# Turning the meta tokens' attention weights on the tensor engine instead of GpSimd and VectorE

## The chip, the cores and the metric

The kernel runs on one core of a Trainium2 chip, in one launch. The time is device microseconds; the figure given for a kernel is the median of its runs, and less is better. A core has a tensor engine (PE; its weight loads are listed apart as PEld), VectorE (DVE), ScalarE (ACT), GpSimd (POOL) and SyncE (SP), which issues the loads and stores. Each engine works through its own instructions in order, and waits for the others by semaphores. PE's results go to PSUM, a small memory of banks; the other engines copy them from there to SBUF.

## The reference, cut to what matters

One layer of a decoder over 512 tokens of width 1024, with 16 learned meta tokens put ahead of them (528 rows). A combined projection feeds a retention mixer, a stick-breaking attention mixer with 16 heads of width 64, and two gates; their merged output goes through an output projection and a gated FFN. The change touches the attention mixer alone:

```python
z = jnp.einsum('bhtd,bhsd->bhts', q_blk, k_pre) * scale
valid = (s_pos[None, :] < t_pos[:, None]) & (s_pos[None, :] >= PAD)
log_not = jnp.where(valid, jax.nn.log_sigmoid(-z), 0.0)
after = lax.cumsum(log_not, axis=3, reverse=True) - log_not
a = jnp.where(valid, jnp.exp(jax.nn.log_sigmoid(z) + after), 0.0)
outs.append(jnp.einsum('bhts,bhse->bhte', a, v_pre))
```

The sum over s runs over the 16 meta tokens and the 512 tokens. The meta tokens' part of it is what the change treats. All is float32.

## The kernel before

**Precision.** A float32 value is held as a pair of values, hi and lo, in the tensor engine's faster float32 type (F32R): `split` (L98) lets ACT copy the value into hi (L99) and DVE subtract hi from it for lo (`lo_of`, L96). A product then is three matmuls: hi by hi, hi by lo, lo by hi. All matmuls are recorded at L90 (`mm`), all transposes on PE at L93 (`turned`); these are matmuls whose stationary operand is the piece that is turned and whose moving operand is the identity.

**The attention stage** (s2, up to about 308 us of the span) walks over eight pairs of heads. For each head and each of four blocks of 128 queries, `score` makes z in a bank of PSUM (`bank_a`), two sigmoids on ACT (L641, L643, tiles sm and sp), a running product on DVE (the scan, L645) and a multiplication on DVE (L646). Its result, sp, holds the weights with queries down the 128 partitions and, along a row, first 16 meta tokens and then the block's tokens (144, 272, 400 or 528 columns).

The weights must be turned before they can be multiplied with the values. For the 512 tokens `turn` does it on PE in blocks of 128x128 into a bank of PSUM (`bank_b`, two banks, tile name pb) and splits the result into ah and al, of 128, 256, 384 or 512 columns. For the 16 meta tokens `turn_meta` does it in another way: GpSimd splits the 16 columns of each block into mg (L654, L655), one DVE instruction turns mg by blocks of 32x32 into x (L656), and GpSimd copies four pieces of x into am (L659). am holds, for both heads of a pair, 32 rows each: 16 of hi and 16 of lo. `values` starts with one matmul of am with vm, the meta tokens' values, and adds those of ah and al with vt; the result is in a `bank_b` too, and ACT (L680) and DVE (L681) move it to ysb.

**vm** is made by `Values.tail`, once for four heads: a projection of xmd, 64 columns that hold the meta tokens' hi, hi, lo, lo, so that the sum of two 32-row halves gives the values twice over; two splits then write 32 rows for each of the two heads of a pair. xmd is filled at the stage's start by four DVE copies. Another tile, xm, with 48 columns (hi, zeros, lo), is filled there as well, for other projections.

**What fills the gaps.** While a pair's attention is made, PE also does the projection for the next pair: q and k by `qk_work` (split on DVE as qa, qb, ka/kl, kb/kl), values (vt) in the pairs 2 to 5, and gates in some pairs. `merge` sets the order: a pair's 20 pieces (four scores z, four turns t, one tm for `turn_meta` and one pv for `values`, for each of the two heads, in the order of `seq`) are emitted one by one, and behind each a share of the projection's columns (`SHARES`). PE executes them in just this order, since `keep` pins it.

**GpSimd's other work.** In the pairs 1 to 5 it computes sums of the tokens' quarters, `token_sums` (tiles go, tl, at L170; six steps behind each tm; ACT makes th at L179), which the gates' products use. In the pairs 6 and 7 it combines the gates' weights in their buffer raw (`quarters_in_place`, L246 to L249). ACT and DVE then split these (wh, wl). The products of the gates are added on DVE into go (L592). All these stand in GpSimd's one queue in the order in which the program emits them, between the steps of `turn_meta`.

Of the kernel before, what the change touches and what calls it, by code (L numbers as in the profile page):

```python
# [10 lines left out]
F32 = mybir.dt.float32  # L11
F32R = mybir.dt.float32r
AF = mybir.ActivationFunctionType
ALU = mybir.AluOpType
PSUM = bass.MemoryType.PSUM

P = 128
NM = 16
T = 512
L = NM + T  # L20
NT = T // P
D = 1024
KD = D // P
RH, DK, DV = 4, 256, 512
SH, DH = 16, 64
# [9 lines left out]
def hybrid_block(  # L35
# [18 lines left out]
    nc = tc.nc  # L54
    x, out = x[0], out[0]
# [9 lines left out]
    def bank_p():  # L65
        return ps_p.tile([P, 512], F32, tag="p", name="pp")
# [4 lines left out]
    def bank_b():  # L71
        return ps_b.tile([P, 512], F32, tag="b", name="pb")
# [5 lines left out]
    ident = cst.tile([P, P], F32, name="ident")  # L78
# [6 lines left out]
    def keep(ins):  # L85

        return tc.keep_in_program_order(ins) if pinned[0] else ins

    def mm(*args, **kw):
        return keep(nc.tensor.matmul(*args, **kw))  # L90

    def turned(dst, src, idn):
        return keep(nc.tensor.transpose(dst, src, idn))  # L93

    def lo_of(lo, src, hi):
        nc.vector.tensor_tensor(lo, src, hi.bitcast(F32), op=ALU.subtract)  # L96

    def split(hi, lo, src):  # L98
        ins = nc.scalar.activation(hi, src, AF.Copy)  # L99
        if split_in_order[0]:  # L100
            tc.keep_in_program_order(ins)
        lo_of(lo, src, hi)
# [233 lines left out]
    hT = hn.tile([P, KD, L], F32R, name="hT")  # L336
    hL = hn.tile([P, KD, L], F32R, name="hL")
    xm = hn.tile([P, KD, 48], F32R, name="xm")
# [94 lines left out]
    with tc.tile_pool(name="s2", bufs=2, side=RS, reuse_waits="tile") as s2:  # L433
# [12 lines left out]
        vms = [s2.tile([P, 4, P], F32R, name=f"vm{i}", bufs=1) for i in range(2)]  # L446
        for vm in vms:
            nc.gpsimd.memset(vm.bitcast(F32), 0.0)
        xmd = s2.tile([P, KD, 64], F32R, name="xmd", bufs=1)
        NS = 3  # L450
        sms = []
        for i in range(NS):
            t = s2.tile([P, L + 2], F32, name=f"sm{i}", bufs=1)
            nc.gpsimd.memset(t[:, L : L + 2], 0.0)
            sms.append(t)
        both = s2.tile([P, T], F32R, tag="am", name="am", bufs=1)
        nc.gpsimd.memset(both.bitcast(F32), 0.0)
        ams = [both[32 * i : 32 * (i + 1)] for i in range(2)]

        vts = {}  # L460

        class Values:
# [18 lines left out]
                    split(vt[:, j, :, 0:DH], vt[:, j, :, DH:], pv)  # L481

            def tail(self, bank=bank_p):
                ps = bank()[:64, :256]
                k = 0
                for wh, wl in self.units:
                    for kk in range(4):
                        mm(ps, xmd[:, k, :], wh[:, kk, :], start=(k == 0), stop=False)
                        mm(ps, xmd[:, k, :], wl[:, kk, :], start=False, stop=(k == KD - 1))
                        k += 1  # L490
                        yield 2 * 256
                vs = s2.tile([32, 256], F32, tag="vs", name="vs", bufs=1)
                nc.scalar.activation(vs, ps[32:64], AF.Copy)
                nc.vector.tensor_tensor(vs, ps[0:32], vs, op=ALU.add)
                vv = vs.rearrange("p (h d) -> p h d", h=4)
                vm = vms[self.c % 2]
                for i in range(2):
                    v = vm[32 * i : 32 * (i + 1)]
                    split(v[:, i::2, 0:DH], v[:, i::2, DH:], vv[:, i::2, :])

            def first(self):
                return (self.load, lambda _: self.part((0, 1)))
# [144 lines left out]
            return sp  # L647

        def turn_meta(hd, att):

            g = s2.tile([P, NT, 32], F32R, tag="mg", name="mg", bufs=1)
            x = s2.tile([P, NT, 32], F32, tag="vs", name="x", bufs=1)
            for i in range(NT):
                nc.gpsimd.tensor_copy(g[:, i, 0:NM], att[i][:, 0:NM])  # L654
                nc.gpsimd.tensor_tensor(g[:, i, NM:], att[i][:, 0:NM], g[:, i, 0:NM].bitcast(F32), op=ALU.subtract)  # L655
            nc.vector.transpose(x.rearrange("p a b -> p (a b)"), g.rearrange("p a b -> p (a b)").bitcast(F32))  # L656
            am = ams[hd].rearrange("p (i b r) -> p i b r", i=NT, b=4)
            for b in range(4):
                nc.gpsimd.tensor_copy(am[:, :, b, :], x[32 * b : 32 * (b + 1)])  # L659

        def turn(j, att):
            w = T - j * P
# [26 lines left out]
        def pair(p):  # L689
# [9 lines left out]
            def tm(hd, j):  # L699
                turn_meta(hd, att[hd])  # L700

                if 1 <= p < 6:
                    for _ in range(6):
                        next(token_sums, None)
# [33 lines left out]
        def innorm(i):  # L738
            n = NM if i == NT else P
            c0 = 0 if i == NT else NM + i * P  # L740
            xt = xts[i]
            junk = bank_a().rearrange("p a b -> p (a b)")
            ss = cst.tile([P, 1], F32, name=f"ss{i}")
            nc.scalar.activation(junk[:n], xt[:n], AF.Square, accum_out=ss[:n])
            rstd_of(ss[:n], ss[:n], 1e-6, 1.0 / D, n)
            for j in range(2):
                hx = s2.tile([P, 512], F32, tag="qb", name="hx")
                cs = slice(512 * j, 512 * (j + 1))
                nc.vector.scalar_tensor_tensor(hx[:n], xt[:n, cs], ss[:n], gps[:n, j, :], op0=ALU.mult, op1=ALU.mult)
                pt = bank_b().rearrange("p (a b) -> p a b", a=4)  # L750
                for a in range(4):
                    turned(pt[:, a, :n], hx[:n, a * P : (a + 1) * P], ident[:n, :n])
                ks = slice(4 * j, 4 * j + 4)
                split(hT[:, ks, c0 : c0 + n], hL[:, ks, c0 : c0 + n], pt[:, :, :n])
# [19 lines left out]
        for j in range(NT):  # L774
# [2 lines left out]
                    pass  # L777
            if j + 2 <= NT:
                innorm(j + 2)
        for i, v in enumerate((hT, hT, hL, hL)):  # L780
            nc.vector.tensor_copy(xmd[:, :, 16 * i : 16 * (i + 1)], v[:, :, 0:NM].bitcast(F32))
        nc.vector.memset(xm[:, :, 16:32].bitcast(F32), 0.0)
        nc.vector.tensor_copy(xm[:, :, 0:16], hT[:, :, 0:NM].bitcast(F32))
        nc.vector.tensor_copy(xm[:, :, 32:48], hL[:, :, 0:NM].bitcast(F32))
# [36 lines left out]
    with tc.tile_pool(name="s3", bufs=1, side=RS, reuse_waits="tile") as s3:  # L821
# [10 lines left out]
        for f in range(0, KD, 2):  # L832
# [4 lines left out]
            for e in range(2):  # L837
                ps = bank_p()
# [95 lines left out]
    def ret_qk(h):  # L934
        uq = feat_units(w_in[:, O_RQ + DK * h : O_RQ + DK * (h + 1)])
        pq = bank_a()
        for e in range(2):
            feat_mm(pq[:, e, :], uq[e], xtok, ltok)
        q = [(qk_tile(), qk_tile()) for _ in range(2)]
        idf = lambda t: t[:, :T]  # L940
        rotate(pq[:, 0, :], pq[:, 1, :], cosT[:, NM:], sinT[:, NM:], idf, [(a[:, :T], b[:, :T]) for a, b in q])
        uk = feat_units(w_in[:, O_RK + DK * h : O_RK + DK * (h + 1)])
        pks = []
        for e in range(2):
            pk = bank_a()
            for i in range(2):
                cs = slice(264 * i, 264 * (i + 1))
                feat_mm(pk[:, i, :264], uk[e], lambda k: hT[:, k, cs], lambda k: hL[:, k, cs])
            pks.append(pk[:, :, :264])
        k = [(qk_tile(), qk_tile()) for _ in range(2)]  # L950
        two = lambda t: t.rearrange("p (a b) -> p a b", a=2)
        rotate(pks[0], pks[1], two(cosT), two(sinT), two, [(two(a), two(b)) for a, b in k])
        return q, k
# [92 lines left out]
    for h in range(RH):  # L1046
        q, k = ret_qk(h)
# [8 lines left out]
        else:  # L1056
# [4 lines left out]
            for f in range(0, KD, 2):  # L1061
# [8 lines left out]
                for e in range(f, f + 2):  # L1070
                    if e < NGE:
                        nc.sync.dma_start(ga[e], ga_d[:, e, :])
                    else:
                        (u,) = feat_units(w_in[:, O_GA + P * e : O_GA + P * (e + 1)])
                        ps = bank_p()
# [22 lines left out]
    with tc.tile_pool(name="s6w", bufs=4, side=RS, reuse_waits="tile") as s6w, tc.tile_pool(  # L1098
        name="s6t", bufs=2, side=RS, reuse_waits="tile"
# [88 lines left out]
    with tc.tile_pool(name="s7", bufs=2, side=RS, reuse_waits="tile") as s7:  # L1188
        for f2 in range(NPF):
            if f2 == 0:  # L1190
                for e in range(2):
                    f = 2 * f2 + e
                    ps = early[f]
# [118 lines left out]
```

## Time and profile before

| | us |
|---|---|
| median of 3 runs (1228.42 to 1229.15) | 1228.53 |
| the profiled execution | 1228.66 |
| its span, first to last instruction | 1226.9 |
| mean granted clock of PE, of full speed | 0.993 |
| attention stage, 62 to 310 us: PE busy | 228.94 |
| DVE busy there | 207.34 |
| GpSimd busy there | 141.50 |

The profile shows one execution. PE, PEld, DVE, ACT and POOL are the engines above; "busy" is the time in which an engine has an instruction under way, and matmuls overlap, so that the distance from one start to the next is what a matmul holds the engine for. A row of the groups reads: line, engine, operation, output and inputs by the program's names, shapes and count; then busy time and mean ns of one; then the idle time of the engine just before them and what ended it. A row of the waits reads: engine, the tile and line that waited, whose work it waited for; total us, times, longest. A row of the timeline begins with the start and the duration in us. Releasers are inferred.

### The profile page before, as it was taken

The page shows a single profiled execution, that of the slowest core. Times are in us where ns is not written, and L with a number is a line of the kernel's source. Part 1 is how long each engine was busy: PE and PEld are TensorE (multiplying, and loading weights), DVE is VectorE, ACT ScalarE, POOL GpSimd, SP SyncE. Part 2 cuts the span into 40 slices and gives each one's busy share as a digit, 9 for nine tenths or more (in the row PEclk, how much of TensorE's full clock was granted, in tenths as well). Part 3 has the DMA queues.
Part 4 walks back from the last instruction along what each step waited for, and adds up shares of the span by engine and source line. Part 5 has one row for each costly group of instructions (what it writes and reads, how often), then busy time and mean ns, then how long its engine had stood idle before and what let it go on. Part 6 is the DMA issues. An engine that isn't in the chain of part 4 may idle for free.

```text
span 1226.9 us, 18829 instructions
## 1 busy us (share of the span) xinstructions
PE 1172.9 (96%) x7597; PEld 1063.2 (87%) x7597; DVE 884.1 (72%) x1133; ACT 532.8 (43%) x869; POOL 390.9 (32%) x425
## 2 busy tenths in 40 slices
PE   7999999889999999989999999999989999999997
PEld 7888888788889988988898899778979999998886
DVE  5588888887537885586678657776799999984333
ACT  5476666655423435342342424334354444443221
POOL 2037767553033210230212020000555666730000
PEclk9999999999999999999999999999999999999999
DMA  6331112114633213122321424424223333343211
GB/s 191 87 95 44 52 52 62 43 44 154 224 130 104 70 59 122 46 97 70 106 70 44 137 69 147 136 88 153 70 69 104 104 104 104 104 158 134 80 58 68
DMA packets 94503, 118.23 MB, mean 96 GB/s; under 512 B 2489, under 2 KB 71105, under 8 KB 94417
## 3 DMA queue, kind: packets, MB, share of 16 engines
q1 hardware_dynamic: 93984, 115.98, 29.2%
q8 instruction: 59, 0.97, 0.3%
q10 hardware_dynamic: 432, 1.07, 0.3%
q14 instruction: 28, 0.22, 0.1%
HBM read 109.96 MB, written 7.08 MB: 95 GB/s over the span
## 4 chain that ended last, share of the span: by engine, by line
PE 70%; DVE 14%; issue 4%; ACT 3%; POOL 3%; DMA 2%; DVEq 0%; POOLq 0%; ACTq 0%; SPq 0%
PE pp L90 30%; PE pb L90 18%; PE pa L90 16%; PE pc L90 4%; DVE wl L96 3%; DVE sm L645 2%; DVE sp L646 2%; PE pb L93 2%; DVE sl L96 1%; ACT wh L99 1%; POOL mg L654 1%; DMA raw<-in_w_in_dram 1%; DVE kl L96 1%; DMA raw<-in_w_sb_out_dram 1%; DMA raw<-in_w_ffn_in_dram 1%
## 5 line engine op out<-in xcount | busy, mean ns | idle before, releaser
L96 DVE TENSOR_TENSOR wl<-raw,wh 128x1024 fp32r<-128x1024 f32 (+1 forms) x202 | 275.2, 1371 | 81.1 <-ACT wh L99 77.8
L99 ACT ACTIVATE wh<-raw 128x1024 fp32r<-128x1024 f32 (+1 forms) x202 | 201.2, 1007 | 255.2 <-PE pp L90 85.5
L90 PE MATMUL pp<-hT,wh 128*128 128x512 f32 (+2 forms) x308 | 109.3, 355 | 13.0 <-DVE qb L96 8.1
L90 PE MATMUL pp<-hL,wh 128*128 128x512 f32 (+2 forms) x308 | 104.0, 338 | 0.0
L90 PE MATMUL pp<-hT,wl 128*128 128x512 f32 (+2 forms) x308 | 103.9, 337 | 0.0
L90 PE MATMUL pp<-qk,wh 128*128 128x512 f32 x256 | 83.1, 399 | 2.0 <-ACT qk L99 1.7
L96 DVE TENSOR_TENSOR wl<-st,wh 128x1024 fp32r<-128x1024 f32 x54 | 80.2, 1490 | 6.6 <-ACT wh L99 6.5
L90 PE MATMUL pp<-wh,hT 128*128 128x256 f32 (+1 forms) x240 | 78.0, 326 | 2.1 <-DVE kl L96 1.4
L90 PE MATMUL pp<-wh,hL 128*128 128x256 f32 (+1 forms) x240 | 76.6, 319 | 0.8 <-DVE ss L142 0.8
L90 PEld LDWEIGHTS pp<-hT,wh 128*128 128x128 f32 x308 | 58.6, 190 | 20.2 <-issue 10.2
L90 PE MATMUL pp<-wl,hT 128*128 128x256 f32 (+1 forms) x240 | 76.1, 317 | 0.0
L99 ACT ACTIVATE wh<-st 128x1024 fp32r<-128x1024 f32 x54 | 55.8, 1054 | 44.5 <-POOL st L279 17.1
L277 POOL TENSOR_TENSOR st<-raw 128x1024 f32<-128x1024 f32 x7 | 17.3, 2470 | 166.6 <-DMA raw<-in_w_in_dram 166.6
L143 POOL TENSOR_TENSOR rs<-rs,nhalf 128x1 f32<-128x1 f32 x20 | 12.2, 612 | 181.4 <-DVE rs L142 181.4
L654 POOL CAST mg<-sp 128x16 fp32r<-128x16 f32 x64 | 31.1, 486 | 109.4 <-DVE sp L646 53.6
L90 PEld LDWEIGHTS pp<-hT,wl 128*128 128x128 f32 x308 | 58.5, 190 | 6.1
L90 PEld LDWEIGHTS pp<-hL,wh 128*128 128x128 f32 x308 | 58.8, 191 | 3.8
L645 DVE TENSOR_TENSOR_SCAN sm<-sm,mask 128x528 f32<-128x528 f32 (+1 forms) x64 | 59.7, 946 | 2.6 <-ACT sm L641 2.1
L90 PE MATMUL pa<-hL,wh 128*128 128x264 f32 (+1 forms) x192 | 61.6, 321 | 0.0
L90 PE MATMUL pa<-hT,wl 128*128 128x264 f32 (+1 forms) x192 | 61.6, 321 | 0.0
L90 PE MATMUL pa<-hT,wh 128*128 128x264 f32 (+1 forms) x192 | 61.6, 321 | 0.0
L90 PEld LDWEIGHTS pp<-qk,wh 128*128 128x128 f32 x256 | 47.6, 188 | 13.4 <-ACT qk L99 2.4
(341 smaller groups left out, 3855.2 us busy)
## 6 DMA issues: line engine op xcount, KB each, us to landing
raw<-in_w_in_dram SPq DMA_DIRECT2D x31, 1024.0 KB, 5.0
raw<-in_w_ffn_in_dram SPq DMA_DIRECT2D x22, 1024.0 KB, 5.1
raw<-in_w_in_dram SPq DMA_DIRECT2D x26, 512.0 KB, 4.2
raw<-in_w_ffn_out_dram SPq DMA_DIRECT2D x11, 1024.0 KB, 5.0
raw<-in_w_ret_out_dram SPq DMA_DIRECT2D x8, 1024.0 KB, 5.1
raw<-in_w_sb_out_dram SPq DMA_DIRECT2D x4, 1024.0 KB, 7.4
raw<-in_w_out_dram SPq DMA_DIRECT2D x4, 1024.0 KB, 5.1
ysb<-in_x_dram SPq DMA_DIRECT2D x4, 512.0 KB, 8.9
```

The lines of the kernel that those rows point to most:

```text
L90: return keep(nc.tensor.matmul(*args, **kw))
L93: return keep(nc.tensor.transpose(dst, src, idn))
L96: nc.vector.tensor_tensor(lo, src, hi.bitcast(F32), op=ALU.subtract)
L99: ins = nc.scalar.activation(hi, src, AF.Copy)
L143: nc.gpsimd.tensor_tensor(dst, dst, nhalf[:n], op=ALU.pow)
L277: nc.gpsimd.tensor_tensor(y, A11, A21, op=ALU.subtract)
L645: nc.vector.tensor_tensor_scan(rev, rev, mask[:, r0:][:, ::-1], 0.0, op0=ALU.mult, op1=ALU.max)
L646: nc.vector.tensor_tensor(sp, sp, sm[:, r0 + 1 : L + 1], op=ALU.mult)
L654: nc.gpsimd.tensor_copy(g[:, i, 0:NM], att[i][:, 0:NM])
```

## The change

`turn_meta` takes a bank of PSUM (`bank_b`) and turns the four pieces of 128x16 on PE, each into 16 rows by 128 columns; `split` then writes the hi rows of am (ACT) and its lo rows (DVE), straight from PSUM. GpSimd's casts, subtractions and copies and the DVE transpose are gone. [...]

```diff
-        xmd = s2.tile([P, KD, 64], F32R, name="xmd", bufs=1)
...
-        ams = [both[32 * i : 32 * (i + 1)] for i in range(2)]
+        ams = [both[64 * i : 64 * i + 48] for i in range(2)]
...
             def tail(self, bank=bank_p):
-                ps = bank()[:64, :256]
+                ps = bank()[:48, :256]
...
-                        mm(ps, xmd[:, k, :], wh[:, kk, :], start=(k == 0), stop=False)
-                        mm(ps, xmd[:, k, :], wl[:, kk, :], start=False, stop=(k == KD - 1))
+                        mm(ps, xm[:, k, :], wh[:, kk, :], start=(k == 0), stop=False)
+                        mm(ps, xm[:, k, :], wl[:, kk, :], start=False, stop=(k == KD - 1))
...
-                vs = s2.tile([32, 256], F32, tag="vs", name="vs", bufs=1)
-                nc.scalar.activation(vs, ps[32:64], AF.Copy)
-                nc.vector.tensor_tensor(vs, ps[0:32], vs, op=ALU.add)
+                vs = s2.tile([NM, 256], F32, tag="vs", name="vs", bufs=1)
+                nc.scalar.activation(vs, ps[32:48], AF.Copy)
+                nc.vector.tensor_tensor(vs, ps[0:NM], vs, op=ALU.add)
...
-                    v = vm[32 * i : 32 * (i + 1)]
-                    split(v[:, i::2, 0:DH], v[:, i::2, DH:], vv[:, i::2, :])
+                    for r in (0, 32):
+                        v = vm[64 * i + r : 64 * i + r + NM]
+                        split(v[:, i::2, 0:DH], v[:, i::2, DH:], vv[:, i::2, :])
...
         def turn_meta(hd, att):
-
-            g = s2.tile([P, NT, 32], F32R, tag="mg", name="mg", bufs=1)
-            x = s2.tile([P, NT, 32], F32, tag="vs", name="x", bufs=1)
+            pm = bank_b()[:NM]
             for i in range(NT):
-                nc.gpsimd.tensor_copy(g[:, i, 0:NM], att[i][:, 0:NM])
-                nc.gpsimd.tensor_tensor(g[:, i, NM:], att[i][:, 0:NM], g[:, i, 0:NM].bitcast(F32), op=ALU.subtract)
-            nc.vector.transpose(x.rearrange("p a b -> p (a b)"), g.rearrange("p a b -> p (a b)").bitcast(F32))
-            am = ams[hd].rearrange("p (i b r) -> p i b r", i=NT, b=4)
-            for b in range(4):
-                nc.gpsimd.tensor_copy(am[:, :, b, :], x[32 * b : 32 * (b + 1)])
+                turned(pm[:, i * P : (i + 1) * P], att[i][:, 0:NM], ident)
+            split(ams[hd][0:NM], ams[hd][32:48], pm)
...
-        for i, v in enumerate((hT, hT, hL, hL)):
-            nc.vector.tensor_copy(xmd[:, :, 16 * i : 16 * (i + 1)], v[:, :, 0:NM].bitcast(F32))
```

So PE has 64 transposes more, in 16 groups of four; GpSimd has 64 casts, 64 subtractions and 64 copies less; DVE loses 16 transposes and the four copies and gains 16 subtractions for am and 8 for vm; ACT gains 16 and 8 casts. On SP two rows change places: in the last pair a load of weights (raw) now stands ahead of the second store of gates. All differences of order lie in the attention stage.

On PE, at the first head's `turn_meta` of pair 2 (pp is a bank of the projection; a row in brackets names the engines that it waits for), there stood before

```order
L90 MATMUL pp<-hT,wh 128x264
L90 MATMUL pp<-hL,wh 128x264
L90 MATMUL pp<-hT,wl 128x264
L90 MATMUL pp<-hT,wh 128x264 [waits DVE_49,PE_49]
L90 MATMUL pp<-hL,wh 128x264
L90 MATMUL pp<-hT,wl 128x264
```

and now

```order
L90 MATMUL pp<-hT,wh 128x264
L90 MATMUL pp<-hL,wh 128x264
L90 MATMUL pp<-hT,wl 128x264
L93 MATMUL pb<-ident,sp 16x128 [waits DVE_49]
L93 MATMUL pb<-ident,sp 16x128 x3
L90 MATMUL pp<-hT,wh 128x264
L90 MATMUL pp<-hL,wh 128x264
L90 MATMUL pp<-hT,wl 128x264
```

The four transposes of 16 columns stand ahead of the matmul that waited for DVE, and the wait is now theirs: they need a bank whose last user, a turn of 256 columns, DVE must have read. So it is in the pairs 1, 2, 4 and 6; in the others the transposes stand behind that matmul.

On DVE, from pair 2's first two kl (lo of k, for the next pair) to its first head's ysb, there stood before

```order
L96 TENSOR_TENSOR kl_136<-pp,ka 64x264
L96 TENSOR_TENSOR kl_139<-pp,kb 64x264
L96 TENSOR_TENSOR al<-pb,ah 128x512
L645 SCALAR_TENSOR_TENSOR sm_132<-sm_132,mask 128x144
L646 TENSOR_TENSOR sp<-sp,sm_132 128x144
L96 TENSOR_TENSOR wl<-raw,wh 128x1024
L656 STREAM_TRANSPOSE x<-mg 128x128
L96 TENSOR_TENSOR kl_136<-pp,ka 64x264
L96 TENSOR_TENSOR kl_139<-pp,kb 64x264
L681 TENSOR_TENSOR ysb<-pb,ysb 64x512
```

and now (the changed kernel's lines and its numbers of buffers)

```order
L96 TENSOR_TENSOR kl_135<-pp,ka 64x264
L96 TENSOR_TENSOR kl_138<-pp,kb 64x264
L96 TENSOR_TENSOR am<-pb,am 16x512
L96 TENSOR_TENSOR al<-pb,ah 128x512
L646 SCALAR_TENSOR_TENSOR sm_131<-sm_131,mask 128x144
L647 TENSOR_TENSOR sp<-sp,sm_131 128x144
L96 TENSOR_TENSOR wl<-raw,wh 128x1024
L96 TENSOR_TENSOR kl_135<-pp,ka 64x264
L96 TENSOR_TENSOR kl_138<-pp,kb 64x264
L676 TENSOR_TENSOR ysb<-pb,ysb 64x512
```

x is gone from between wl and the second pair of kl, and the lo half of am stands right behind the first pair of kl. An x of the pair before's second head, which stood early in the pair (between an al of 128 columns and the sp of 528 columns, ahead of qb), is gone too; that head's am now stands behind the pair's ysb, between the turns of 384 and 512 columns.

In the last pair, GpSimd's steps L246 to L249 follow each other without the steps of mg between them.

## The prediction

> **What bounds the kernel now.** The page's first part comes first: the tensor engine (PE) is busy for 96% of the span, so on the whole its instructions, and the waits between them, make the time.
>
> ```profile
> PE 1172.9 (96%) x7597; PEld 1063.2 (87%) x7597; DVE 884.1 (72%) x1133; ACT 532.8 (43%) x869; POOL 390.9 (32%) x425
> ```
>
> The change touches only the attention stage, so the second view is the table of windows for that stage alone, from 62 to 310 us. Its columns are the window, its length, then busy time (and count) of PE, the weight loads PEld, DVE, ACT and POOL, the granted clock, the DMA share and GB/s.
>
> ```profile
> 62.00:310.00 248.00, 228.94 (x1538) 208.02 (x1537) 207.34 (x327) 157.89 (x342) 141.50 (x260) 0.99 0.23 72
> ```
>
> PE is busy for 228.9 of 248.0 us, so some 19 us are idle; DVE is busy for 207.3, close behind. The third view, PE's waits from 56 to 310 us, says who ends that idle time:
>
> ```profile
> PE pp L90 <- DVE qb L96: 6.9, 7, 1.8
> PE pp L90 <- DVE kl L96: 4.8, 5, 1.4
> PE pb L93 <- DVE al L96: 2.8, 3, 1.1
> PE pb L93 <- DVE ysb L681: 2.3, 5, 0.7
> PE pp L90 <- DVE go L592: 1.2, 1, 1.2
> PE pp L90 <- DVE wl L96: 0.8, 1, 0.8
> PE pb L93 <- DVE sp L646: 0.7, 1, 0.7
> PE pp L90 <- ACT wh L99: 0.4, 1, 0.4
> ```
>
> They add up to 19.9 us, and all but 0.4 end on DVE. So a pair of heads is a chain of two stretches. From the pair's start DVE sets the pace, through qb, the two pairs of kl and the first head's ysb; behind that ysb PE sets it (four turns of the second head, its values), and DVE waits for ACT and PE. GpSimd is not in that list. Is it in the chain at second hand? The view of the tile am, which GpSimd fills, ends like this:
>
> ```profile
> who waited for it (us, times):
> busy tenths in 40 slices 0011211020000000000000000000000000000000
> ```
>
> Nobody is listed between the two lines: no matmul waits for am. GpSimd holds others up only through mg, for which DVE's transpose x waits. That is the first row to price.
>
> **What goes.** In the groups, x is 16 transposes:
>
> ```profile
> L656 DVE STREAM_TRANSPOSE x<-mg 128x128 f32<-128x128 f32 x16 | 5.0, 310 | 4.2 <-POOL mg L655 4.0
> ```
>
> Busy 5.0 us and idle before it 4.2: 9.2 us of DVE's time, or 0.575 a head. GpSimd loses
>
> ```profile
> L654 POOL CAST mg<-sp 128x16 fp32r<-128x16 f32 x64 | 31.1, 486 | 109.4 <-DVE sp L646 53.6 <-PE pa L90 45.8 <-ACT wh L99 9.9
> L659 POOL CAST am<-x 32x128 fp32r<-32x128 f32 x64 | 27.6, 432 | 10.6 <-DVE x L656 8.5
> L655 POOL TENSOR_TENSOR mg<-sp,mg 128x16 fp32r<-128x16 f32 x64 | 24.0, 380 | 3.1
> ```
>
> that is 82.7 of its 141.5 us, which is worth nothing by itself: it was beside the chain. What it does to DVE is a rival below.
>
> **What comes: PE.** 64 transposes in groups of four. No transpose of 16 columns is in the trace; the nearest are four of 128 columns:
>
> ```profile
> 111.47 0.39 PE L90 MATMUL pp<-hT,wl 128*128 128x512 f32 x1
> 111.69 0.60 PE L93 MATMUL pb<-ident,sp 128*128 128x128 f32 x4
> 112.05 0.47 PE L90 MATMUL pp<-hT,wh 128*128 128x512 f32 x1
> 112.36 0.39 PE L90 MATMUL pp<-hL,wh 128*128 128x512 f32 x1
> ```
>
> The group holds PE from 111.69 to 112.05, 0.36 us, and the next matmul takes 0.31 to its successor where others of its form take 0.23: 0.08 more. So 0.44 us a group, 16 groups, 7.0 us. From below a group may cost nothing where PE waits anyway; from above 0.66 (the busy time of four in the last such row below), 10.6 in all. I take 0.44, since the moving side, 128 columns of the identity, is the same.
>
> The Trainium skill, in "VectorE: DVE Perf Modes", section "The three transpose paths", speaks against the change: a DVE transpose by 32x32 blocks is given 311 ns and a TensorE transpose 390 ns. The first agrees with the 310 ns of the x row. By the second, as an estimate from that page, 64 transposes would be 25 us and the sum some 18 us higher; the row above shows four in 0.36 us one behind the other, and the measurement decides.
>
> **What comes: DVE and ACT.** 16 subtractions am of 16x512 from PSUM. Free size sets the time of such rows: the nearest is
>
> ```profile
> L681 DVE TENSOR_TENSOR ysb<-pb,ysb 64x512 f32<-64x512 f32 x16 | 11.0, 689 | 5.7 <-ACT ysb L680 5.3
> L99 ACT ACTIVATE ah<-pb 128x512 fp32r<-128x512 f32 x16 | 9.5, 595 | 12.8 <-PE pb L93 12.8
> ```
>
> so 0.69 us each, 11.0 in all; bounds 0 (behind PE's part) and 11.0. ACT gets 16 casts of 0.60, 9.5 us; it is busy for 158 of 248 us, and these stand beside DVE's work. The tail writes vm in four pieces instead of two, so two more subtractions and two more casts for each group of four heads:
>
> ```profile
> 46.75 0.61 DVE L96 TENSOR_TENSOR vm<-vs,vm 32x128 fp32r<-32x128 f32 x2 [0.43 <-ACT vm L99]
> ```
>
> 0.30 each, 0.6 a tail. Two tails run inside the DVE-paced part (for the pairs 4 and 6): +1.2. Two run at the stage's start, where the four casts to xmd go; there the late qa and qb meet a wait that is already there:
>
> ```profile
> 59.27 0.47 PE L90 MATMUL pp<-hT,wh 128*128 128x512 f32 x1 [1.00 <-DVE kl L96]
> ```
>
> between 0 and 4 x 0.30 = 1.2; I take 0.2.
>
> **The sum, pair by pair.** Pair 2 shows how these meet.
>
> ```profile
> 125.89 0.69 DVE L96 TENSOR_TENSOR qb<-pp,qb 64x512 fp32r<-64x512 f32 x1
> 126.62 0.42 DVE L96 TENSOR_TENSOR al<-pb,ah 128x256 fp32r<-128x256 f32 x1
> 126.73 0.36 PE L90 MATMUL pp<-hT,wh 128*128 128x264 f32 x1 [0.65 <-DVE qb L96]
> 131.71 0.36 PE L90 MATMUL pp<-wh,hT 128*128 128x256 f32 x1 [1.15 <-DVE kl L96]
> 137.39 0.43 DVE L96 TENSOR_TENSOR al<-pb,ah 128x256 fp32r<-128x256 f32 x1
> 137.49 0.49 PE L93 MATMUL pb<-ident,sp 128*128 128x128 f32 x3
> ```
>
> The first head's four transposes now stand ahead of the matmul at 126.73 and need a bank of PSUM, whose last user is read by the al of 256 columns, one place behind qb on DVE. So PE's wait for qb becomes a wait for that al (end 127.04, 0.45 later as DVE's pace stands), plus 0.44 of transposes. Behind the transposes on PE are the projection's matmuls, then the matmul that waits 1.15 us for kl: the 0.89 fits in that. DVE's own stretch in a pair loses the x of the pair before's second head and of its own first head (2 x 0.575 = 1.15) and gains the first am, 0.69, ahead of ysb: -0.46. In PE's stretch the second head's four transposes come right behind the three at 137.49 and their bank is free when the al at 137.39 ends, at 137.82, about when they are due (three take some 0.25): 0.44 and 0.1 of wait. Its am stands beside PE's values. So a pair costs -0.46 + 0.54 = +0.08, and seven pairs +0.6.
>
> **The last pair** is different: its projection is gates whose weights GpSimd combines in place, and mg stands between these steps.
>
> ```profile
> 282.66 0.20 POOL L654 CAST mg<-sp 128x16 fp32r<-128x16 f32 x1 [0.50 <-DVE sp L646]
> 282.81 1.29 POOL L247 TENSOR_TENSOR raw<-raw 128x512 f32<-128x512 f32 x1
> 284.06 0.64 POOL L655 TENSOR_TENSOR mg<-sp,mg 128x16 fp32r<-128x16 f32 x1
> 304.84 0.66 PE L93 MATMUL pb<-ident,sp 128*128 128x128 f32 x4 [0.79 <-DVE al L96]
> ```
>
> Without mg those steps, and the loads that wait for their buffer, come earlier. PE's waits there are 1.2 (go), 0.8 (wl), 0.4 (wh) and 0.8 (the last row): 3.2 us at most. Against it the second head's transposes cost 0.44, and they stand earlier on PE than the turn at 304.84, at the same wait. I take -1.0, about a third; bounds -3.2 and +0.44. Also, SP now starts a load of weights ahead of the second store of gates; the load is what is waited for, the store is not.
>
> Sum against the profiled execution, 1228.66 (span 1226.9 and 1.8 around it; 0.1 above the median of the runs, 1228.53): +0.6 + 1.2 + 0.2 - 1.0 = +1.0, so **1229.7 us**. A measurement can tell about 0.2%, 2.5 us, from no change: 1226.1 to 1231.0 is "same".
>
> **Rivals.**
>
> *PE pays for all of it (slower).* The sum lets kl and ysb hide the first head's transposes. These waits are 4.8 + 2.3 = 7.1 us, 0.89 a pair; DVE, 0.46 earlier, leaves 0.43 of it, against 0.44 of transposes and up to 0.45 of waiting for the al. It is close: where the wait that is left falls under the transposes and the al's wait, PE's fixed order sets the pace. The full price is 8 x 0.44 = 3.5 and, in the pairs 1, 2, 4 and 6, where the transposes stand ahead of the qb wait, 4 x 0.45 = 1.8: 1229.7 + 5.3 = **1235.0**, with half of it 1232.4. For it: five of eight pairs show a kl wait at all. Against it: where there is one it is 0.96 on the mean (4.8 in 5), which holds the whole 0.89.
>
> *DVE is freed by a quiet GpSimd (faster).* Some rows of DVE are long, on the mean of the stage and (the second row of each form) in the first pair alone:
>
> ```profile
> L645 DVE TENSOR_TENSOR_SCAN sm<-sm,mask 128x400 f32<-128x400 f32 x16 | 18.6, 1161 | 0.0
> L645 DVE TENSOR_TENSOR_SCAN sm<-sm,mask 128x400 f32<-128x400 f32 x2 | 2.0, 980 | 0.0
> L646 DVE TENSOR_TENSOR sp<-sp,sm 128x272 f32<-128x272 f32 x16 | 10.0, 624 | 0.6
> L646 DVE TENSOR_TENSOR sp<-sp,sm 128x272 f32<-128x272 f32 x2 | 0.8, 422 | 0.0
> ```
>
> The excess is 16 x (0.181 + 0.202) = 6.1 us. If it went in proportion to GpSimd's busy time, 82.7/141.5, DVE would win 3.6, and the last pair its whole 3.2 instead of 1.0: 1229.7 - 3.6 - 2.2 = **1223.9**. Against it: in the first pair GpSimd does nothing but mg and am, and there the rows are short. So the token sums (pairs 1 to 5) and the in-place steps (6 and 7) lengthen DVE's work, and these stay; freed of mg they bunch in earlier pairs.
>
> The Trainium skill stands on this rival's side: "SBUF — State Buffer", section "Who interferes with whom", says that DVE and GpSimd share a port pair under an exclusive lock. The first pair's rows speak against counting mg under it.
>
> *The change does nothing to the pace*, GpSimd's work being hidden and PE's falling in waits: 1228.7, within the forecast's band.
>
> **How the numbers follow.** Forecast (with the third rival) 0.45, its own range 1227 to 1231; PE pays at least half 0.32; DVE is freed 0.23. The range goes from the faster rival's price, cut by a little, 1224.5, to just short of the slower one's, 1234.5. Faster by over 0.2% 0.23, same 0.45, slower 0.32.
>
> **What would show it.** Right: PE busy up by about 7 us in the stage and its idle time down by about 6; a group of 16x128 near 0.44 us; am on DVE near 0.69; qb waits replaced by waits of the 16x128 transposes for al; kl waits shorter but there. Wrong: kl and ysb waits gone and the span longer (the first rival); the 400-column scan near 0.98 and the span shorter (the second). A transposed group of 16 columns that costs PE far less or more than 0.44, or an am that stands ahead of qb on DVE, would upset the sum.

## The result and the profile after

The changed kernel takes 1242.28 us (median of 4 runs, 1240.23 to 1243.30) against 1228.79: a ratio of 1.0109 (95% interval 1.0094 to 1.0125), 13.5 us slower. The forecast, 1229.7, and its range, up to 1234.5, were wrong. The profiled execution is the fastest of the four, 1240.23 us, with a span of 1238.4.

First the page's busy times of the changed kernel: PE has its 64 matmuls more, GpSimd 68 us less. That is less than the 82.7 us of work that went: what GpSimd kept became longer.

```profile
PE 1180.6 (95%) x7661; PEld 1068.8 (86%) x7661; DVE 902.0 (73%) x1137; ACT 544.6 (44%) x893; POOL 322.6 (26%) x233
```

To find the stage's loss, take a pair as the time from the end of one pair's second ysb on DVE to the end of the next pair's. In windows cut there (columns as before), the pairs 1, 2 and 3 of the kernel before read

```profile
88.60:116.70 28.10, 26.37 (x159) 22.91 (x159) 22.95 (x38) 18.91 (x42) 19.41 (x36) 1.00 0.17 49
116.70:143.00 26.30, 24.42 (x174) 22.59 (x173) 21.93 (x37) 16.70 (x40) 19.74 (x37) 1.00 0.27 80
143.00:172.30 29.30, 27.55 (x195) 25.49 (x195) 24.58 (x41) 19.53 (x43) 19.99 (x36) 1.00 0.07 19
```

and of the changed kernel

```profile
89.50:121.10 31.60, 27.80 (x163) 24.31 (x163) 27.67 (x37) 19.80 (x44) 14.46 (x14) 0.95 0.14 42
121.10:153.00 31.90, 27.72 (x187) 25.23 (x186) 27.75 (x37) 19.83 (x44) 26.09 (x28) 0.95 0.23 68
153.00:187.20 34.20, 30.64 (x203) 28.45 (x202) 28.22 (x40) 20.73 (x45) 14.54 (x14) 0.90 0.05 16
```

The three pairs are 14.0 us longer, and DVE, with almost the same number of instructions, is busy for 14.2 us more (83.6 against 69.5). Some 2.2 of the 14.2 were expected: six am take 4.1 us there, six x took 1.9. The other five pairs together are 1.5 us longer. So in this execution the attention stage ends 15.4 us later (324.4 against 309.1). All that follows it, which the change leaves as it was, took 3.9 us less (914.0 against 917.9). In the sixteen profiles of this document that rest varies from 910.9 to 917.9 us, so that a stage's sum in one profile gives the whole time only to within a few us.

What became slow on DVE? Three rows of scans and multiplications in the first two of these pairs, and one of al, before,

```profile
L645 DVE TENSOR_TENSOR_SCAN sm<-sm,mask 128x272 f32<-128x272 f32 x4 | 3.1, 766 | 0.0
L646 DVE TENSOR_TENSOR sp<-sp,sm 128x528 f32<-128x528 f32 x4 | 2.8, 694 | 0.0
L645 DVE TENSOR_TENSOR_SCAN sm<-sm,mask 128x144 f32<-128x144 f32 x4 | 1.9, 465 | 0.0
L96 DVE TENSOR_TENSOR al<-pb,ah 128x512 fp32r<-128x512 f32 x4 | 2.8, 692 | 2.5 <-ACT ah L99 2.4
```

and after (lines one further down):

```profile
L646 DVE TENSOR_TENSOR_SCAN sm<-sm,mask 128x272 f32<-128x272 f32 x4 | 5.0, 1251 | 0.0
L647 DVE TENSOR_TENSOR sp<-sp,sm 128x528 f32<-128x528 f32 x4 | 4.0, 1005 | 0.0
L646 DVE TENSOR_TENSOR_SCAN sm<-sm,mask 128x144 f32<-128x144 f32 x4 | 3.4, 851 | 0.0
L96 DVE TENSOR_TENSOR al<-pb,ah 128x512 fp32r<-128x512 f32 x4 | 2.8, 691 | 2.1 <-ACT ah L99 2.0
```

A scan of 272 columns takes 1251 ns instead of 766. What reads one operand from PSUM, like al, kept its time. So did the scans of 528 columns here (1252 ns in both). The timeline of GpSimd says what runs beside it:

```profile
90.30 1.00 POOL L170 TENSOR_TENSOR go<-hL 128x256 f32<-128x256 f32 x1 [60.84 <-ACT sm L642]
...
101.92 3.47 POOL L170 TENSOR_TENSOR tl<-go,th 128x256 fp32r<-128x256 f32 x4 [1.17 <-ACT th L179]
105.46 0.94 POOL L170 TENSOR_TENSOR go<-hT 128x256 f32<-128x256 f32 x1
121.84 1.07 POOL L170 TENSOR_TENSOR go<-hL 128x256 f32<-128x256 f32 x1 [15.44 <-DMA gb_d<-go]
```

In the kernel before the first sum started at 98.4 us, behind am's copies, six at a time with mg between. Now nothing stands ahead of them in GpSimd's queue: they start as the pair starts, and go on in one go for some 16 us, just where DVE has its scans; so again from 121.8 us on, in the pairs 2 and 3.

PE then waits longer (56 to 325 us; the prediction had 2.8 us in 3 waits for al):

```profile
PE pb L93 <- DVE al L96: 17.3, 11, 2.4
PE pp L90 <- DVE go L593: 2.5, 2, 2.2
PE pp L90 <- DVE qb L96: 2.4, 2, 1.5
```

and at three of the long waits the granted clock (third column from the end) falls to a half: in windows of 0.5 us, for about 3.4 us the first two times and for 6.8 the third. The first row is PE's timeline, the others are windows of 4 us:

```profile
103.74 0.60 PE L93 MATMUL pb<-ident,sp 128*16 128x128 f32 x4 [2.42 <-DVE al L96]
```

```profile
104.00:108.00 4.00, 4.00 (x24) 3.98 (x22) 3.88 (x7) 1.42 (x3) 2.32 (x3) 0.58 0.02 4
136.00:140.00 4.00, 4.00 (x24) 4.00 (x23) 3.88 (x7) 1.19 (x2) 3.92 (x5) 0.66 0.16 47
168.00:172.00 4.00, 4.00 (x20) 3.69 (x20) 3.89 (x8) 0.87 (x2) 1.10 (x1) 0.50 0.23 69
```

By the clock's means of the three pairs (0.95, 0.95, 0.90) PE lost about 1.6 + 1.6 + 3.4 = 6.6 us of full clock there (6.8 added up in windows of 0.5 us), part of it beside waits for DVE. The kernel before has one such spell in the stage, of 1.7 us, in pair 4.

### The profile page after: what moved, and what is told of

Same layout as the page of the kernel before. It is cut to its first block, busy times and chain, and to the rows that moved or that the text cites. A ratio compares the mean times of both kernels' runs of the same rounds, so it can differ in the third digit from the quotient of the medians.

```text
span 1238.4 us, 18754 instructions
## 1 busy us (share of the span) xinstructions
PE 1180.6 (95%) x7661; PEld 1068.8 (86%) x7661; DVE 902.0 (73%) x1137; ACT 544.6 (44%) x893; POOL 322.6 (26%) x233
## 3 DMA queue, kind: packets, MB, share of 16 engines
q1 hardware_dynamic: 93984, 115.98, 28.6%
## 4 chain that ended last, share of the span: by engine, by line
PE 77%; DVE 11%; ACT 3%; DMA 3%; issue 3%; POOL 2%; SPq 0%; DVEq 0%; POOLq 0%; ACTq 0%
PE pp L90 35%; PE pb L90 19%; PE pa L90 16%; PE pc L90 4%; DVE wl L96 3%; PE pb L93 3%; DVE sm L646 2%; POOL go L170 2%; ACT wh L99 1%; DVE sl L96 1%; DMA raw<-in_w_in_dram 1%; DVE sp L647 1%; DMA ysb<-in_x_dram 1%; DMA raw<-in_w_sb_out_dram 1%; DVE qb L96 0%
## 5 line engine op out<-in xcount | busy, mean ns | idle before, releaser
L646 DVE TENSOR_TENSOR_SCAN sm<-sm,mask 128x528 f32<-128x528 f32 (+1 forms) x64 | 65.0, 1028 | 1.5 <-ACT sm L642 1.0
L277 POOL TENSOR_TENSOR st<-raw 128x1024 f32<-128x1024 f32 x7 | 17.3, 2471 | 165.8 <-DMA raw<-in_w_in_dram 165.8
L93 PE MATMUL pb<-ident,sp 128*128 128x128 f32 (+1 forms) x224 | 39.9, 287 | 18.9 <-DVE al L96 17.3
```

What stands on the lines that cost most here:

```text
L277: nc.gpsimd.tensor_tensor(y, A11, A21, op=ALU.subtract)
L646: nc.vector.tensor_tensor_scan(rev, rev, mask[:, r0:][:, ::-1], 0.0, op0=ALU.mult, op1=ALU.max)
```

## The experiments

**Theory S**: the token sums, which mg no longer holds back, run in one go beside DVE's scans and lengthen them. **Rival P**: PE pays for the transposes and for two more users of its two banks pb. **Rival A**: ACT stands at th for GpSimd's sums and delays ah. The table gives the pairs of each profiled execution in us (pair 0 from 62 us of the span).

| kernel | 0 | 1 | 2 | 3 | 4 | 5 | 6 | 7 | median us | ratio to before (95%) |
|---|---|---|---|---|---|---|---|---|---|---|
| before | 26.6 | 28.1 | 26.4 | 29.3 | 29.4 | 28.8 | 31.3 | 47.3 | 1228.8 | 1 |
| changed | 27.5 | 31.6 | 31.9 | 34.2 | 28.8 | 27.7 | 32.2 | 48.6 | 1242.3 | 1.0109 (1.0094, 1.0125) |
| paced | 29.9 | 27.4 | 27.9 | 28.3 | 30.1 | 29.8 | 32.1 | 47.7 | 1231.5 | 1.0026 (1.0016, 1.0036) |
| late_sums | 30.3 | 26.5 | 42.2 | 27.7 | 28.9 | 27.7 | 33.2 | 49.5 | 1244.2 | 1.0119 (1.0102, 1.0136) |
| after_no_sums | 37.1 | 26.2 | 26.0 | 27.7 | 28.8 | 27.7 | 32.2 | 48.6 | 1233.5 | 1.0042 (1.0028, 1.0057) |
| before_no_sums | 32.9 | 26.4 | 26.4 | 27.4 | 28.2 | 27.4 | 31.4 | 47.1 | 1229.2 | 1.0012 (1.0001, 1.0023) |
| groups | 28.4 | 26.2 | 26.0 | 29.6 | 30.9 | 31.3 | 34.7 | 48.6 | 1234.6 | 1.0043 (1.0030, 1.0055) |
| before_groups | 27.7 | 26.5 | 26.2 | 31.6 | 31.2 | 30.2 | 35.0 | 48.0 | 1232.6 | 1.0043 (1.0025, 1.0060) |
| double_turn | 29.6 | 27.8 | 28.3 | 29.2 | 30.9 | 30.2 | 32.9 | 47.9 | 1230.9 | 1.0024 (1.0013, 1.0036) |
| turn_in_pp | 31.9 | 31.8 | 33.5 | 33.7 | 34.7 | 33.3 | 36.5 | 46.9 | 1259.3 | 1.0247 (1.0229, 1.0264) |
| start | 26.7 | 27.3 | 27.9 | 28.3 | 30.1 | 29.8 | 32.2 | 48.4 | 1230.4 | 1.0015 (1.0004, 1.0025) |
| sums_12 | 26.9 | 26.2 | 26.0 | 29.3 | 29.5 | 28.8 | 35.3 | 49.2 | 1229.4 | 1.0007 (0.9998, 1.0017) |
| sums_spread | 28.4 | 27.3 | 27.7 | 29.3 | 29.0 | 28.7 | 32.2 | 48.6 | 1229.1 | 1.0015 (1.0004, 1.0025) |
| hold_raw | 27.3 | 27.4 | 27.7 | 29.4 | 29.0 | 28.6 | 32.2 | 49.6 | 1230.8 | 1.0010 (0.9999, 1.0021) |
| hold_pinned | 26.7 | 27.4 | 27.6 | 29.4 | 29.6 | 28.6 | 29.9 | 49.5 | 1228.4 | 1.0000 (0.9991, 1.0009) |
| before_hold | 27.0 | 28.1 | 26.4 | 29.4 | 29.4 | 28.8 | 26.1 | 52.5 | 1228.9 | 1.0010 (1.0001, 1.0019) |

### Holding the sums back again

One GpSimd copy of a single element, tick, ahead of the six steps:

```diff
                 if 1 <= p < 6:
+                    tc.keep_in_program_order(nc.gpsimd.tensor_copy(tick, ams[hd][32:33, 0:1].bitcast(F32)))
                     for _ in range(6):
                         next(token_sums, None)
```

> The changed kernel, with one GpSimd copy of a single element of am ahead of each head's six steps of token sums, so that the sums wait for am as they did for mg before. Theory S (the token sums, which mg no longer holds back, run in one go beside DVE's heavy stretch in the pairs 1 to 3 and lengthen it): most of the 13.5 us goes, 1227 to 1232 us; pairs 1 to 3 lose their 3.5 to 5.5 us each. Rival P (PE pays for 64 transposes and for two more users of its two banks pb): nothing changes for PE, 1239 to 1244. Rival A (ACT stands 1.9 us at th, waiting for GpSimd, and delays ah behind it): as S if th waits less, else as P.

1231.5 us: 10.8 of the 13.5 us are gone, and the pairs 1 to 3 take 83.6 us as before (83.8), not 97.7. Nothing of PE's work was changed, so rival P has at most the rest, 3.1 us. GpSimd's first steps now start where tick lets them:

```profile
106.60 0.17 POOL L700 COPY tick<-am 1x1 f32<-1x1 f32 x1 [86.69 <-DVE am L96]
106.86 0.74 POOL L170 TENSOR_TENSOR go<-hT 128x256 f32<-128x256 f32 x1
```

### The sums left out, in both kernels

```diff
-                if 1 <= p < 6:
-                    for _ in range(6):
-                        next(token_sums, None)
```

These two kernels leave the sums out; in their place, in lines not shown here, th and tl are filled with zeros once.

> The changed kernel without the token sums: th and tl are filled with zeros once, so the gates' products are not the reference's. Theory S: 13 us or more go, 1220 to 1228 us. Rival P: 1236 or more, as only ACT's 4 us for th and a little of DVE go.

> The kernel before without the token sums (zeros in th and tl as above). Theory S: 1220 to 1227 us, and the changed kernel without sums within 3 us of it, as the prediction had it for everything but the sums. Rival P: the changed kernel without sums is 8 us or more above this one.

The totals miss what was expected, for two reasons that lie ahead of pair 1. The two fills of th and tl stand first in GpSimd's queue (3.52 and 3.51 us from 0.87 us on), and the first head's ysb of the kernel before comes 6.4 us later (88.6 against 82.2); and the changed kernel's first ysb comes 3.5 us later still (92.1), of which more below. Pairs 1 to 5 are what was asked for: 136.4 us changed and 135.7 before. So the sums cost 6.2 us there in the kernel before (141.9) and 17.8 in the changed one (154.2), and all else that the change does costs 0.7. For these pairs the forecast had 5 x 0.08 and one tail, +1.0.

### Other places for the sums

```diff
             def pv(hd, j):
                 values(p, hd, aT[hd])
+                if hd == 0 and p < 7:
+                    tc.keep_in_program_order(nc.gpsimd.tensor_copy(tick, ysb[0:1, p, 0:1]))
+                    for _ in range(8):
+                        next(token_sums, None)
```

> The changed kernel, with the token sums moved: eight steps a pair in the pairs 0 to 6, behind the first head's values, held by a copy of one element of ysb. There PE sets the pace and DVE reads PSUM or idles (2.5 to 3.6 us a pair). Theory S: 1222 to 1229 us, better than with the sums at their old place, and perhaps below the kernel before. Rival P: 1238 to 1243.

1244.2 us, 15 us above the range's upper end. The pairs 1, 3, 4 and 5 take about what they take without the sums (26.5 to 28.9 us), pair 6 is 1 us longer than in the changed kernel, and pair 2 takes 42.2. There PE waits, the granted clock falls to 0.5, and ACT's sigmoid of pair 1's gate, which frees PE's bank pp, comes only near the end of pair 2 (161.0):

```profile
129.20 0.56 PE L90 MATMUL pp<-hT,wh 128*128 128x264 f32 x1 [4.31 <-DVE qb L96]
```

```profile
155.90 0.59 ACT L575 ACTIVATE go<-pp 128x512 f32<-128x512 f32 x1
```

A group of sums holds one buffer go from its first step to its last and the other to its sixth. Here the second group has its first two steps from 116.9 us and its sixth at 154.0, in the next pair, and the gate had to wait. PE was then left with one of its two banks pp, and waited for qb, which reads that one; no view names the banks, so this is how I read it. So a group must be whole within a pair, and not in a pair with a gate:

```diff
+                if hd == 0 and 2 <= p < 6:
...
+                    for _ in range(14):
```

> The changed kernel with all 14 steps of one of the four groups of token sums behind the first head's values of each of the pairs 2 to 5, held there by a copy of one element of ysb. In the run with moved sums a group lay over two pairs and kept both buffers go, for which a gate's sigmoid (pair 1) waited with its PSUM bank; here no gate wants go while a group holds it. Theory S: pairs 1 to 5 near their 136.4 us without sums (143.5 in the paced run, 154.2 in the changed kernel), so 1224 to 1229 us. Rival P: no better than the paced run, 1230 to 1234.

> The kernel before with the token sums in the same four places as in the run with groups. Its pairs 1 to 5 take 141.9 us with the sums at the old place and 135.7 without. Theory S: 1223 to 1227 us; the difference to the changed kernel with groups is then what the turning itself costs, forecast at +1.0, and 0 to 4 us by the runs without sums. Rival P: the changed kernel with groups is 8 us or more above this one.

Neither met it: 1234.6 and 1232.6. Pairs 1 and 2 are at their best, but 14 steps with th in between reach well into the next pair, whose scans they lengthen. Against the runs without sums the pairs 3 to 6 are 3 to 4 us longer each in the kernel before and 2 to 4 in the changed one. The profile of before_groups is of an execution of 1237.8 us, 5 above the median, and has four spells of low clock in these pairs, so that a part of its 3 to 4 us is the clock. Still, this placing leaves both kernels 0.4% above the kernel before, whichever engine turns the weights. The difference between the two medians, 2 us, is inside what the runs without sums allowed.

### What the transposes cost PE

```diff
+            for _ in range(2):
                 for i in range(NT):
                     turned(pm[:, i * P : (i + 1) * P], att[i][:, 0:NM], ident)
```

> The paced run's kernel with each of the 64 transposes of 16 columns done twice, into the same place. If PE pays for every group of four (16 x 0.44), 7 us above the paced run's 1231.5: 1238.5. If only the second heads' groups are paid, as the prediction had it, 3.5 us: 1235. If all of it falls in waits, 1231.5.

```diff
-            pm = bank_b()[:NM]
+            pm = bank_p()[:NM]
```

> The paced run's kernel with the 64 transposes in a bank of pp instead of pb, so that the turns of 512 columns no longer wait for the turn just ahead of them. Rival P: 2 to 4 us faster than the paced run's 1231.5. Theory S, by which pb's order is a small matter: within 2 us of it, or slower where the projection now waits for its banks.

Twice the transposes: 1230.9, as the paced kernel. The groups of PE (first the changed kernel, then this one) show that they were done:

```profile
L93 PE MATMUL pb<-ident,sp 128*16 128x128 f32 x64 | 10.5, 291 | 9.2 <-DVE al L96 9.2
```

```profile
L93 PE MATMUL pb<-ident,sp 128*16 128x128 f32 x128 | 16.6, 273 | 5.1 <-DVE al L96 5.0
```

Their idle time falls as their busy time grows. In the profiled execution the pairs 1 to 6 grow by 3.6 us, about the 3.5 of the second heads; but what follows the stage is 3.4 us shorter there, in the medians nothing is left of it, and the intervals leave room for some 1.6 us. By either, PE's price is no cause of 13.5 us. In a bank of pp the same transposes cost 28 us: the projection needs that bank, and PE's waits of that kernel are now

```profile
PE pp L90 <- DVE kl L96: 13.4, 4, 3.4
PE pp L93 <- DVE kl L96: 5.9, 3, 2.1
```

with seven spells of low clock beside them, 18.8 us of full clock in all, so that most of the 28 us can be the clock. pb was the right bank, and rival P falls.

### The stage's start

```diff
+        pinned[0] = True
-        for v in vals:
-            for _ in v.tail(bank_b):
-                pass
+        for _ in vals[0].tail(bank_b):
+            pass
+        for _ in range(KD):
+            work.step()
+        for _ in vals[1].tail(bank_b):
+            pass
         work.drain()
         half = None
-        pinned[0] = True
```

> The paced run's kernel, and at the stage's start the second tail's matmuls stand behind the first pair's q projection instead of ahead of it, with PE's order pinned. In the profiles of the changed kind PE idles there 2.3 to 2.5 us for qb (1.15 before) and in most of them the granted clock falls to about 0.6 of full for 4 us right behind it. If that idle time and the clock behind it make the rest of the paced run's +3.1 us, the first head's ysb comes at 82 to 83 us instead of 84.9 and the time is 1227 to 1229.5. If the rest lies elsewhere, 1231 to 1232.

The first ysb comes at 81.7 us instead of 84.9, a little better than expected; the median falls by 1.1 only, to 1230.4, above the 1227 to 1229.5 that went with it, so that the rest of the paced kernel's +3 is at most in part there. What a spell of low clock costs shows by itself in two profiles that idle alike ahead of it, to 56.2 us (paced) and 56.1 (groups):

```profile
56.00:60.00 4.00, 3.78 (x20) 3.81 (x21) 2.16 (x4) 2.29 (x5) 0.00 (x0) 0.61 0.43 121
```

```profile
56.00:60.00 4.00, 3.89 (x28) 3.78 (x29) 2.08 (x3) 2.36 (x5) 0.00 (x0) 1.00 0.47 136
```

The first, paced, has the spell and its first ysb at 84.9; the other has none and 83.4: 1.5 us, about what (1 - 0.61) x 4 gives.

### Fewer sums at a time, and the in-place steps

On the same start, 12 steps a pair from pair 2 on; then the first group in pair 1 behind am and the others in the pairs 2 to 5:

> The same start; the token sums 12 steps a pair behind the first head's values, in the pairs 2 to 6, so that less of them reaches into the next pair's DVE stretch than with 14 in one group. Theory S: the pairs 2 to 6 cost less than in the run with groups (29.6 to 34.7 us from pair 3 on), 1226 to 1230 us. If holding go over two pairs or what still reaches into the next stretch costs as much, 1231 to 1235.

> As the run with 12 steps a pair, but the first group stands in pair 1 (6 steps behind the first head's am, 8 behind the second's) and the other three in the pairs 2 to 5, so that nothing of the sums is left beside GpSimd's in-place steps at the start of pair 6, where the run with 12 steps had three subtractions vm of 16x128 take 3.99 us and PE idle 4.1 us with the clock at half behind it. Theory S: pair 6 back from 35.3 to about 32.2 us, pair 1 up from 26.2 to about 27.3: 2 us less, 1227.5, at or below the kernel before. If pair 6 stays at 35, the in-place steps alone do it: 1229 to 1231.

1229.4 and 1229.1: by the ratios (1.0007 and 1.0015, against 1.0015 at this start) the placing is worth 1 us or nothing, inside the noise, and neither beats the kernel before. The first spoils pair 6 (35.3): what is left of the sums delays GpSimd's in-place steps into the vm of the tail, and PE then waits 4.13 us for al, with a spell of low clock twice as long as usual. DVE and GpSimd there:

```profile
235.89 3.99 DVE L96 TENSOR_TENSOR vm<-vs,vm 16x128 fp32r<-16x128 f32 x3
```

```profile
235.19 1.83 POOL L247 TENSOR_TENSOR raw<-raw 128x512 f32<-128x512 f32 x1
237.10 1.29 POOL L248 TENSOR_TENSOR raw<-raw 128x512 f32<-128x512 f32 x1
```

Three subtractions of 128 columns take 1.33 us each, as long as a GpSimd step. The in-place steps run ahead too, and without th or go, so they tell whether it is the running ahead as such. They were held by a tick in their turn:

```diff
+        if hold:
+            hold.pop()()
-        nc.gpsimd.tensor_tensor(A22, A21, A22, op=ALU.add)
+        tc.keep_in_program_order(nc.gpsimd.tensor_tensor(A22, A21, A22, op=ALU.add))
```

with `hold` a copy of pair 6's ysb ahead of the first set, the other three steps pinned alike; in hold_raw without the pins.

> The run with spread sums, and GpSimd's first in-place steps on raw (L246 to L249 of the kernel before), which now run at the start of pair 6 beside the scans, are held by a copy of one element of ysb until pair 6's first head is done. In pair 6 the scans and multiplications take 13.6 us of DVE, 10.8 where GpSimd is idle. Theory S, carried over to these steps: pair 6 falls from 32.15 by up to 2.8 us, the time from 1229.1 to 1226 to 1227, below the kernel before. If the loads and splits that wait for raw then come too late in pair 7 (48.6 us), what is won in pair 6 is lost there: 1228.5 to 1231.

> As the run before it, with GpSimd's order of the in-place steps pinned, since there the first set still stood ahead of the copy that was to hold it and ran at 232 us, beside the scans. Theory S: pair 6 falls from 32.2 by up to 2.8 us (scans and multiplications from 13.6 to about 10.8 us), the time from about 1229.5 to 1226.5 to 1227.5. If the splits that wait for raw come too late in pair 7 (48.6 to 49.6 us), no gain: 1229 to 1231.

> The kernel before with the same hold on the first in-place set and nothing else. There pair 6 takes 31.3 us with 13.5 of scans and multiplications. Theory S: the same 2 to 3 us, 1225.5 to 1227, since what lengthens DVE is not mg; by the faster rival of the prediction (mg itself lengthens DVE) less, 1227.5 or more. If pair 7 takes it back: 1228 to 1230.

hold_raw held nothing: the first set, at 232.10 us, still stood ahead of its tick at 256.07, and its 1230.8 us say nothing on the question. Pinned, the set runs at 250 us, and DVE's rows in pair 6 are, without the hold (sums_spread),

```profile
L646 DVE TENSOR_TENSOR_SCAN sm<-sm,mask 128x528 f32<-128x528 f32 x2 | 3.4, 1686 | 0.0
L96 DVE TENSOR_TENSOR vm<-vs,vm 16x128 fp32r<-16x128 f32 x4 | 2.2, 552 | 0.1
```

and with it

```profile
L650 DVE TENSOR_TENSOR_SCAN sm<-sm,mask 128x528 f32<-128x528 f32 x3 | 3.7, 1247 | 0.0
L96 DVE TENSOR_TENSOR vm<-vs,vm 16x128 fp32r<-16x128 f32 x4 | 1.1, 281 | 0.1
```

The first head's part of pair 6 shrinks from 24.7 to 18.9 us, in the kernel before from 24.4 to 18.7. This is not all a gain: of the 6.2 to 6.3 us that DVE's busy time falls there, about 4.0 are the same instructions made shorter, in either kernel, and 2.4 are two wl of 1024 columns, which stand behind the held steps and now come later (from 259 us on in before_hold, 245 and 251 before). With all of mg still there (before_hold) the scans of 528 columns take 1244 ns, as without mg (1242). That settles it: GpSimd's large operations beside DVE's scans are the cause, in either kernel, and mg's small ones no visible part of it; nor is rival A needed, as these steps have no th.

In the time little of it is left. In the kernel before the pairs 6 and 7 take 78.6 us with and without the hold: pair 7 has those wl and longer waits for the gates, 52.5 us instead of 47.3, and the 1228.9 us fall under "If pair 7 takes it back". In the changed kernel the two take 79.4 us instead of 80.7. Its 1228.4 us, ratio 1.0000, are the best of the changed kernels: level with the kernel before.

## Why the prediction was wrong

**What bounds the stage** held: DVE sets the pace up to the first ysb, and am has no waiter but its own lo half.

**The step that failed** is the one on GpSimd: 82.7 us gone are "worth nothing by itself", and of the sums "these stay; freed of mg they bunch in earlier pairs". The place was right and the price was missing: I carried DVE's durations over unchanged. mg was slow and light, and by its order in GpSimd's queue it spread the sums over five pairs. The rows for it were there (scans of 1161 against 980 ns, 272-column multiplications of 624 against 422), and I used them only to argue against a gain. The price is 11.6 us (17.8 against 6.2 in the pairs 1 to 5), in which the clock's spells are included (6.8 us of full clock in the changed kernel's pairs 1 to 5, 1.7 in the kernel before).

**PE's transposes**: 0.45 us a group where 0.44 was estimated (103.74 to 104.10, and 0.09 behind it). That the first heads' fall in waits held, and of the second heads' 3.5 us little or nothing reaches the medians. The waits moved as forecast, away from qb (6.9 to 2.4 us) to al, but those for al grew to 17.3 us, since DVE came later. One of the five kl waits that the prediction counted, at 59.27 us, lies ahead of pair 0, so four pairs show one and not five. The rival that PE pays for it all, with the highest chance but one, is refuted by the doubled and the paced runs, though the time came out on its side.

**DVE's terms**: am 0.68 us each (0.69 forecast). Pair 4, with a tail, costs 28.8 us without sums in the changed kernel and 28.2 in the kernel before, the 0.6 of the tail's price. And the pairs 1 to 5 without sums, +0.7 where +1.0 was forecast, say that in these pairs the forecast's sum was right for all but the token sums.

**The start**: forecast +0.2, and in the changed kernel's profile the first ysb is 0.2 later. But PE idles 2.45 us there instead of 1.15, and where a spell of low clock follows, as in the paced profile, it costs 1.5 more. I had not thought of the clock at all.

**The last pair**: forecast -1.0, and +1.3 came. The first head's part is 1.2 shorter, as forecast; then a new order on DVE loses it. Before, go stood ahead of a wl that waits for a load:

```profile
294.88 0.42 DVE L592 TENSOR_TENSOR go<-pp,go 128x256 f32<-128x256 f32 x1 [0.44 <-PE pp L90]
...
296.72 1.29 DVE L96 TENSOR_TENSOR wl<-raw,wh 128x1024 fp32r<-128x1024 f32 x1 [1.19 <-ACT wh L99]
```

and now behind it, so that PE waits 2.21 us for go:

```profile
309.31 1.23 DVE L96 TENSOR_TENSOR wl<-raw,wh 128x1024 fp32r<-128x1024 f32 x1 [2.96 <-ACT wh L99]
310.45 0.42 DVE L593 TENSOR_TENSOR go<-pp,go 128x256 f32<-128x256 f32 x1
```

I had read the new order for PE and for the turns, not to the end of DVE's queue.

**The faster rival** was right that GpSimd lengthens DVE's work and wrong in that this went with GpSimd's busy time: 68 us less of it made DVE slower.

What stays open: how the 11.6 us divide between DVE's longer instructions and the clock behind PE's longer waits (6.8 us of full clock lost against 1.7, in part hidden), and the 1 to 2 us by which the changed kernel with held sums still lies above the kernel before.

## What to carry to other kernels

Before taking work off an engine that nobody waits for, ask what that work holds back in its queue: an in-order queue paces what stands behind it, and with the pace gone the rest runs as early as its buffers let it. Give such work a place on purpose (a tiny copy that reads the right tile is enough, 0.17 us here), and see that it holds no buffer that others want. A stretch where the neighbour engine reads PSUM or waits looks best, but here it was worth at most about 1 us over the old place with a tick. And an idle gap of PE can have a second price: the clock may drop with it.

## What the runs showed of the hardware

DVE instructions with two operands in SBUF can stretch beside a large GpSimd instruction: 281 ns to 1.33 us for a 16x128 subtraction, 1247 to 1686 ns for a scan of 528 columns. Those with an operand in PSUM did not (al of 512 columns, 692 and 691 ns). It can also fall on GpSimd: a sum, 0.73 us elsewhere, took 1.77 at 97.81 us of the changed kernel, beside a scan of 528 columns that kept its 1.25. The Trainium skill, "SBUF — State Buffer", section "Who interferes with whom", gives the reason: a shared port pair under an exclusive lock. The rows agree for the large GpSimd operations. For mg's 16 columns DVE lost next to nothing (its rows in the first pair were short, and its scans of 528 columns with the hold took 1244 ns with mg and 1242 without), while mg's casts took from 191 to 1202 ns: there it seems to be GpSimd that waited.

PE's granted clock fell to a half for 3.4 us, or for twice that, in every spell of the sixteen profiles' attention stages, so that a spell costs 1.7 us of full clock. Most came with idle gaps of 1.4 to 4.5 us; in three profiles (sums_spread at 73 us, hold_raw at 71.5, before_hold at 277.5) the longest gap just ahead was under 1 us. Not each gap had one: of two alike at 56 us one was followed by a spell and one not, and the changed kernel's 2.45 us at 55 us had none either. The Trainium skill, "TensorE: Matmul & The Clock Gate", section "Why this matters for your kernels", warns of idle gaps over about 3 us; here shorter ones were enough.
